# A planner's account of GpSimd and accumulator reads, and the buffers of memory attention, in a two-block transformer kernel

## Chip, cores and metric

The kernel runs on one core of one Trainium2 chip, as one program. The metric is the time of one execution in microseconds of the device, in the median of the runs.

## What is computed

Two transformer blocks, one after the other, in float32, on 256 tokens of width 1024. The first block has two layers, the second has one. Each layer is a mixer and a feed-forward part, each with its RMS norm before it and its residual addition after it.

```python
for layer in range(2):                                   # first block
    u = rms_norm(x, attn_norm_w[layer]) @ w_in[layer]
    o_main = silu(g) * rms_norm(retention(q, k, v))      # layer 0: six heads
    o_main = rms_norm(diff_attention(q, k, v, lam))      # layer 1: q and k normed per 64 columns
    qc = rms_norm(u[..., 3 * MAIN_WIDTH:])               # 4 heads of 64, normed per head
    mk = rms_norm(mem_part_k);  o_mem = softmax(qc @ mk.T / 8) @ mv
    x = x + concat(o_main, o_mem) @ w_out[layer]
    gu = rms_norm(x, ffn_norm_w[layer]) @ w_gate_up[layer]
    x = x + (silu(gu[:FFN]) * gu[FFN:]) @ w_down[layer]
# second block: a state-space mixer and a forgetting attention side by side
# (16 heads each, q and k normed per head), then a gated MLP with a short convolution
```

The memory attention of the two layers of the first block attends from the 256 tokens to 256 memory rows, with four heads.

## The kernel before

**Products.** Every large product is made in three passes of a split: the weights are cast to fp32r (`wh`, on ACT) and the rest is subtracted (`wl`, on VectorE), the activations likewise (`lth`, `ltl`). A unit of weights has 256 rows and 512 columns: one DMA into one of four stage buffers (`st`), one cast, one subtraction. `mm3` issues the three matmuls of one step of 128 rows. Projections accumulate in PSUM banks of the pool `psm` (three of them). All small products, transposes through TensorE and attention use the pool `psa`, which has five banks.

**Stages.** Mixer 0 (retention and memory attention), feed-forward 0, mixer 1 (differential attention and memory attention), feed-forward 1, mixer 2 (state space and forgetting attention), feed-forward 2. In a mixer, the projections of the input run in a fixed order of column chunks (`ORDER0`, `ORDER1`, `ORDER2`), and all the small work of the heads is woven between their matmuls. At the end `w_out` accumulates the output projection over pairs of 128 rows in the order `OUT0`, `OUT1` or `OUT2`, waiting for each pair's heads.

**The planner.** The program is written out by a planner in Python, which decides the order of the instructions before anything runs. `Weave` (line 100 onwards) keeps a modelled clock for each engine; each call to an engine goes through `note` (line 133), which starts the operation at the latest of its engine's clock and its operands' modelled ends and adds `cost` (line 116). Small work is a `Task`, a Python generator. A `yield` hands control back: with nothing, the task may go on at the modelled end of what it has just issued; with a ring and a number, once so many buffers of that ring are free; with tasks, once these are done. `poll` (line 200) runs, after each three matmuls of a projection, all steps whose time has come by the account (100 ns late at the soonest). `join` (line 208) moves TensorE's clock on until the tasks asked for are done. `fill` (line 382) issues weight loads as stage buffers come free, and the casts and subtractions when their operands are there by the account and either the unit is next in turn or ACT's (VectorE's) clock is no more than 100 ns ahead of TensorE's. On the chip each engine takes its instructions in the order in which they were written; semaphores make it wait where an operand is late.

**Rings.** A ring is a set of buffers. A buffer taken with `get(True)` is held until `close`; a free one comes with the modelled end of its last use.

**GpSimd.** Reciprocal roots run on GpSimd, as a tensor_scalar (scale and epsilon) and a tensor_tensor with the power -1/2 (`rsqrt`, line 282, and `stat`, line 479). Tiles with one column (`s1n`) belong to the large norms, with four (`s4r`) to `head_norm` (line 989), with eight (`s8r`) to the memory's keys (`mk`) and queries (`u`), with sixteen (`s16r`) to the heads of differential and forgetting attention (`uq`, `aug`), with two (`s2r`) to the state-space part. In `group_norm64` (line 594) and `head_norm`, a multiplication on VectorE waits for the root, and transposes on TensorE wait for the multiplication.

**ACT's accumulators.** An activation with `accum_out` appears in the profile as two records, the ACTIVATE and an ACTIVATION_READ_ACCUMULATOR. The attentions' exponentials and the squares of the norms have it.

**Memory attention** (`mem_attn`, line 686). After the norm and transposes of the queries, two blocks of 128 tokens run as two tasks, the second started 2.5 us of the account after the first. A block takes two `psa` banks, makes the scores of four heads, takes for each half a buffer of the ring `mpr` (tile `mp`, two buffers in both mixers), writes the exponentials there with their sums, divides, and transposes each half through TensorE into `mpT`, giving back its buffer. When both blocks are done, the product with `mv` follows and its result is split for the output projection.

In the profile all of this has line 89, the helper through which every operation is recorded. The tiles' names tell the operations apart.

Of the kernel before, what the change touches and what calls it, by code (L numbers as in the profile page):

```python
# [10 lines left out]
ALU = mybir.AluOpType  # L11
# [88 lines left out]
class Weave:  # L100
# [15 lines left out]
    def cost(self, key, op, args, kw, aps):  # L116
        n = max(a.size() // a.shape[0] if callable(a.size) else a.size // a.shape[0] for a in aps[:2])
        if key == "T":
            if op == "transpose":
                return 109  # L120
            return n / 2.4 + 3 if args[2].dtype == F32R else max(n / 0.6, 104) + 3
        if key == "V":
            return 65 + 1.05 * n + 60 * any(a.size() == a.shape[0] if callable(a.size) else a.size == a.shape[0] for a in aps[1:])
        if key == "S":
            c = 45 + 0.88 * n + 93 * sum(isinstance(kw.get(k), bass.AP) for k in ("bias", "scale", "accum_out"))
            func = args[2] if op == "activation" else None
            if func in (AF.Exp, AF.Silu) and func != self.table:
                self.table = func
                c += 1280
            return c  # L130
        return 230 + 170 * n if kw.get("op") == ALU.pow else 120 + 2 * n

    def note(self, key, op, args, kw):
        aps = [x for x in list(args) + list(kw.values()) if isinstance(x, bass.AP)]
# [88 lines left out]
def _build(tc, a, out, stop):  # L223
# [13 lines left out]
    def ring(p, n, tag, bufs, dtype=F32):  # L237
        return Ring(W, p, [P] + (list(n) if isinstance(n, (tuple, list)) else [n]), dtype, tag, bufs)
# [103 lines left out]
    def g64(ap):  # L342
        return ap.rearrange("p (g d) -> p g d", d=64)
# [250 lines left out]
    def group_norm64(sq, srcs, dsts, ng):  # L594

        ns = len(srcs)
        ss = small([P, ns, ng], "g")
        for i, s_ in enumerate(srcs):
            yield sq, 1
            q = sq.get(True)  # L600
            S.activation(g64(q[:, : 64 * ng]), s_, AF.Square)
            yield
            V.tensor_reduce(ss[:, i, :], g64(q[:, : 64 * ng]), axis=AX.X, op=ALU.add)
            sq.close(q)
        yield
        r = rsqrt(ss.rearrange("p a b -> p (a b)"), ns * ng, 1.0 / 64)
        yield
        for i in range(ns):
            V.tensor_tensor(dsts[i], srcs[i], bcast(r[:, i * ng : (i + 1) * ng], 64), op=ALU.mult)
        yield  # L610
# [75 lines left out]
    def mem_attn(l, mx, got, kvt, qc, oT, mpr):  # L686

        yield [got]
        qg = [g64(q_) for q_ in qc]
        yield from group_norm64(sqm[0], qg, qg, 4)  # L690
        yield psa, 1
        ps = psa.get(True)
        transposes(ps, [qc[t][:, p * P : (p + 1) * P] for p in range(2) for t in range(2)])
        yield
        qT = mx.tile([P, 2, 256], F32, tag="mqT", name=W.name("mqT"))
        S.activation(qT[:].rearrange("p a b -> p (a b)"), ps[:], AF.Copy, scale=pc(C_MQ + l))
        psa.close(ps)
        yield [kvt]
        v, kT = kvt.val
        sums = small([P, 2, 4], "m")  # L700
        pT = mx.tile([P, 2, 4, 256], F32, tag="mpT", name=W.name("mpT"))

        def block(t):
            yield psa, 2
            sc = [psa.get(True), psa.get(True)]
            for p in range(2):
                for j in range(2):
                    T.matmul(sc[j][:, p * 256 : (p + 1) * 256], qT[64 * j : 64 * j + 64, p, t * P : (t + 1) * P],
                             kT[64 * j : 64 * j + 64, p, :], start=True, stop=True)
            prs = []  # L710
            yield
            for j in range(2):
                mxv = small([P, 2])
                V.tensor_reduce(mxv, sc[j][:].rearrange("p (j m) -> p j m", j=2), axis=AX.X, op=ALU.max)
                V.tensor_scalar(mxv, mxv, -0.125, None, op0=ALU.mult)
                yield mpr, 1
                pr = mpr.get(True)
                for p in range(2):
                    S.activation(pr[:, p * 256 : (p + 1) * 256], sc[j][:, p * 256 : (p + 1) * 256], AF.Exp,
                                 bias=mxv[:, p : p + 1], scale=0.125, accum_out=sums[:, t, 2 * p + j : 2 * p + j + 1])  # L720
                psa.close(sc[j])
                prs.append(pr)
            yield
            rs = small([P, 4])
            V.reciprocal(rs, sums[:, t, :])
            yield
            for j in range(2):
                for p in range(2):
                    cols = slice(p * 256, (p + 1) * 256)
                    S.activation(prs[j][:, cols], prs[j][:, cols], AF.Copy, scale=rs[:, 2 * p + j : 2 * p + j + 1])  # L730
            yield
            for j in range(2):
                yield psa, 1
                tp = psa.get(True)
                transposes(tp, blocks(prs[j]))
                mpr.close(prs[j])
                S.copy(pT[:, j, :, t * P : (t + 1) * P], g128(tp[:]))
                psa.close(tp)
            yield

        b0 = go(block(0))
        yield 2500
        b1 = go(block(1))
        yield [b0, b1]
        yield psa, 1
        ps = psa.get(True)
        for p in range(2):
            for mb in range(2):
                for j in range(2):
                    h = (2 * p + j) * 64  # L750
                    T.matmul(ps[64 * j : 64 * j + 64, p * 256 : (p + 1) * 256], v[mb][:, h : h + 64], pT[:, j, 2 * p + mb, :],
                             start=mb == 0, stop=mb == 1)
        yield
        lt = yield from lt_tiles()
        yield from split(lt[0][:], lt[1][:], ps[:])
        psa.close(ps)
        for t in range(2):
            for p in range(2):
                oT[6 + p, t] = tuple(z[:, (2 * p + t) * P : (2 * p + t + 1) * P] for z in lt)
        yield  # L760
        return [lt]
# [246 lines left out]
    def mixer0(H, nxt, first):  # L1008
        scope = ExitStack()
        mx = scope.enter_context(tc.tile_pool(name="m0", bufs=1))  # L1010
        w = a["w_in"][0]
        u, E, oT = {}, {}, {}
        dtab = mx.tile([P, 6, 384], F32, name="dtab")
        sTr, hsq, onr, mpr = ring(mx, 384, "sT", 3), ring(mx, 512, "hsq", 1), ring(mx, 512, "on", 3), ring(mx, 512, "mp", 2)
        sqm[0] = ring(mx, 256, "sqm", 2)

        def chunk(c, ev, first=None):
# [112 lines left out]
    def mixer1(H, nxt, kv1):  # L1130
        scope = ExitStack()
        mx = scope.enter_context(tc.tile_pool(name="m1", bufs=1))
# [1 line left out]
        oT, u, qkT, E = {}, {}, {}, {}  # L1134
        btab = mx.tile([P, 384], F32, name="btab")
        uqr, sqg, pdr, aTr = ring(mx, 512, "uq", 4), ring(mx, 512, "sqg", 1), ring(mx, 384, "pd", 6), ring(mx, 384, "aT", 5)
        hsq, onr, mpr = ring(mx, 512, "hsq", 1), ring(mx, 512, "on", 2), ring(mx, 512, "mp", 2)
        sqm[0] = ring(mx, 256, "sqm", 1)

        def chunk(c, serial=False):  # L1140
# [748 lines left out]
```

## Time and profile before

| | |
|---|---|
| runs, median (lowest to highest) | 1014.52 us (1013.83 to 1016.05), 3 runs |
| the profiled execution: its own time | 1014.46 us |
| its span, first to last instruction | 1012.5 us |
| TensorE busy | 1002.2 us, 99% |
| VectorE busy | 678.1 us, 67% |
| ACT busy | 622.5 us, 61% |
| GpSimd busy | 69.8 us, 7%, 93 instructions |
| HBM | 191 GB/s over the span |

Busy times are of one profiled execution. A record of a matmul overlaps with the next one's, so the distance of two begins is the time that a matmul takes from TensorE's queue, and not the record's length. Idle time is time in which no record of an engine runs. TensorE is called PE, VectorE DVE and GpSimd POOL in the profile.

### The profile page before, as it was taken

To read this page: it belongs to the slowest core of one execution; us is meant where nothing else is said; L and a number is where in the kernel's file an instruction comes from. 1 tells how busy PE (TensorE), PEld (TensorE's weight loads), DVE (VectorE), ACT (ScalarE), POOL (GpSimd) and SP (SyncE) were. 2 spreads that over 40 slices of the span, in tenths; PEclk is the share of its full clock that TensorE was granted. 3 is DMA by queue.
4 is the path that set the end of the run, shared out by engine and by line. 5 is a ranking of instruction groups with operands and counts; after the bars stand their busy time and mean duration, and the time that the engine had idled before them with its cause. 6 is when DMAs were issued, how large, how long until landed. Compare 5 with 4: busy or idle time off the path is not lost.

```text
span 1012.5 us, 13836 instructions
## 1 busy us (share of the span) xinstructions
PE 1002.2 (99%) x4994; PEld 832.4 (82%) x4994; DVE 678.1 (67%) x1026; ACT 622.5 (61%) x1001; POOL 69.8 (7%) x93
## 2 busy tenths in 40 slices
PE   8999999999999999999999999999999999999998
PEld 6887888888898777788888888888888888888887
DVE  5675666555556877756565477778767667878775
ACT  7558654443455887644445356688778557767853
POOL 1121000000001231100000001100400010000000
PEclk9999999999999999999999999999999999999999
DMA  7763566776564433677677457633632659877743
GB/s 250 261 222 105 183 208 212 252 229 193 179 227 155 146 104 107 208 247 233 203 229 239 137 152 220 215 104 104 210 125 84 208 164 289 262 232 240 247 156 116
DMA packets 121780, 193.79 MB, mean 191 GB/s; under 512 B 8400, under 2 KB 39920, under 8 KB 121584
## 3 DMA queue, kind: packets, MB, share of 16 engines
q1 hardware_dynamic: 121712, 192.92, 59.9%
q8 instruction: 39, 0.64, 0.3%
q14 instruction: 29, 0.24, 0.1%
HBM read 183.43 MB, written 9.45 MB: 191 GB/s over the span
## 4 chain that ended last, share of the span: by engine, by line
PE 91%; ACT 2%; DVE 2%; DMA 2%; POOL 2%; issue 1%; SPq 0%; ACTq 0%; DVEq 0%
PE psm L89 60%; PE psa L89 31%; POOL s8r L89 1%; DMA xt<-x 1%; ACT pd L89 1%; DMA dc<-am 1%; DMA st<-w_gate_up 1%; DVE wl L89 0%; DVE pd L89 0%; DVE s L89 0%; ACT wh L89 0%; POOL s4r L89 0%; POOL s16r L89 0%; SPq L259 0%; ACT qkT L89 0%
## 5 line engine op out<-in xcount | busy, mean ns | idle before, releaser
L89 DVE TENSOR_TENSOR wl<-st,wh 128x1024 fp32r<-128x1024 f32 (+2 forms) x339 | 388.4, 1166 | 195.4 <-ACT wh L89 194.5
L89 ACT CAST wh<-st 128x1024 fp32r<-128x1024 f32 (+2 forms) x339 | 334.5, 1007 | 223.9 <-PE psm L89 84.0
L89 PE MATMUL psm<-wh,lth 128*128 128x512 f32 (+2 forms) x1024 | 395.2, 386 | 1.1 <-ACT lth L89 1.1
L89 PE MATMUL psm<-wl,lth 128*128 128x512 f32 (+2 forms) x1024 | 385.6, 377 | 0.0
L89 PE MATMUL psm<-wh,ltl 128*128 128x512 f32 (+2 forms) x1024 | 381.0, 377 | 0.3 <-DVE ltl L89 0.2
L89 PEld LDWEIGHTS psm<-wh,ltl 128*128 128x128 f32 x1024 | 192.6, 188 | 36.8 <-DVE ltl L89 0.9
L89 PEld LDWEIGHTS psm<-wh,lth 128*128 128x128 f32 x1024 | 192.8, 188 | 35.8 <-issue 2.0
L89 PEld LDWEIGHTS psm<-wl,lth 128*128 128x128 f32 x1024 | 192.9, 188 | 32.6 <-DVE wl L89 0.7
L89 PE MATMUL psa<-wh,lth 128*128 128x512 f32 x328 | 130.7, 398 | 0.0
L89 PE MATMUL psa<-wl,lth 128*128 128x512 f32 x328 | 127.9, 390 | 0.0
L89 PE MATMUL psa<-wh,ltl 128*128 128x512 f32 x328 | 105.1, 390 | 0.0
L89 PEld LDWEIGHTS psa<-wh,ltl 128*128 128x128 f32 x328 | 61.6, 188 | 13.2
L89 PEld LDWEIGHTS psa<-wh,lth 128*128 128x128 f32 x328 | 61.6, 188 | 12.4 <-ACT lth L89 0.3
L89 PEld LDWEIGHTS psa<-wl,lth 128*128 128x128 f32 x328 | 61.7, 188 | 12.0 <-issue 0.2
L89 POOL TENSOR_SCALAR s1n<-s1n 128x1 f32<-128x1 f32 x14 | 5.6, 402 | 461.6 <-ACT sq L89 461.4
L89 DVE SCALAR_TENSOR_TENSOR cc<-na,ccol,cc 128x255 f32<-128x255 f32 (+1 forms) x64 | 27.4, 480 | 7.4 <-ACT cc L89 7.2
L89 ACT ACT_TABLE_LOAD x20 | 25.7, 1283 | 7.8 <-DMA dc<-am 2.8
L89 DVE SCALAR_TENSOR_TENSOR sg<-psm,s1n,sg 128x512 f32<-128x512 f32 (+1 forms) x24 | 16.9, 705 | 19.5 <-PE psm L89 19.3
L89 ACT ACTIVATE uu<-psm,s1n 128x512 f32<-128x512 f32 (+1 forms) x24 | 15.6, 652 | 18.3 <-PE psm L89 18.2
L89 ACT ACTIVATE sg<-psm,s1n 128x512 f32<-128x512 f32 (+1 forms) x24 | 15.7, 653 | 17.9 <-PE psm L89 17.7
L89 ACT ACTIVATE sq<-xt 128x512 f32<-128x512 f32 x24 | 15.2, 634 | 18.2 <-DVE xt L89 17.7
L89 POOL TENSOR_TENSOR s16r<-s16r,mhalf 128x16 f32<-128x16 f32 x7 | 22.2, 3166 | 0.6
(213 smaller groups left out, 829.3 us busy)
## 6 DMA issues: line engine op xcount, KB each, us to landing
st<-w_gate_up SPq DMA_DIRECT2D x80, 512.0 KB, 4.6
st<-w_in SPq DMA_DIRECT2D x67, 512.0 KB, 4.3
st<-w_down SPq DMA_DIRECT2D x66, 512.0 KB, 5.5
st<-w_up SPq DMA_DIRECT2D x40, 512.0 KB, 4.8
st<-w_out SPq DMA_DIRECT2D x32, 512.0 KB, 3.9
scr<-sq SPq DMA_DIRECT2D x64, 128.0 KB, 4.8
fl<-scr SPq DMA_DIRECT2D x16, 512.0 KB, 5.9
st<-w_in SPq DMA_DIRECT2D x30, 256.0 KB, 3.8
```

What stands on the lines that cost most here:

```text
L89: f(*args, **kw)
```

## The change

Three edits. In `cost`, an ACT operation with `accum_out` costs 110 ns more; a GpSimd power goes from 230+170n to 380+175n ns for n columns; any other GpSimd operation goes from 120+2n to 450+15n, but for a memset, which costs 120. In `mem_attn`, a block asks for two buffers of `mpr` before it asks for its two banks, where it asked for one buffer at a time after its scores and the maximum. The ring has three buffers in mixers 0 and 1. The program's instructions stay; the planner writes them in the order of the new account.

```diff
@@ Weave.cost
         if key == "S":
             c = 45 + 0.88 * n + 93 * sum(isinstance(kw.get(k), bass.AP) for k in ("bias", "scale", "accum_out"))
+            c += 110 * ("accum_out" in kw)
             func = args[2] if op == "activation" else None
...
-        return 230 + 170 * n if kw.get("op") == ALU.pow else 120 + 2 * n
+        return 380 + 175 * n if kw.get("op") == ALU.pow else 120 if op == "memset" else 450 + 15 * n
@@ mem_attn
         def block(t):
+            yield mpr, 2
+            prs = [mpr.get(True), mpr.get(True)]
             yield psa, 2
             sc = [psa.get(True), psa.get(True)]
...
-            prs = []
             yield
             for j in range(2):
                 mxv = small([P, 2])
...
-                yield mpr, 1
-                pr = mpr.get(True)
+                pr = prs[j]
...
                 psa.close(sc[j])
-                prs.append(pr)
@@ mixer0
-        ..., mpr = ..., ring(mx, 512, "mp", 2)
+        ..., mpr = ..., ring(mx, 512, "mp", 3)
@@ mixer1
-        hsq, onr, mpr = ring(mx, 512, "hsq", 1), ring(mx, 512, "on", 2), ring(mx, 512, "mp", 2)
+        hsq, onr, mpr = ring(mx, 512, "hsq", 1), ring(mx, 512, "on", 2), ring(mx, 512, "mp", 3)
```

## Rows read from the trace of the kernel before

**Rows 1.** The page's head and its first part: busy time of TensorE, share of the span, instructions.

```profile
span 1012.5 us, 13836 instructions
...
PE 1002.2 (99%) x4994; PEld 832.4 (82%) x4994; DVE 678.1 (67%) x1026; ACT 622.5 (61%) x1001; POOL 69.8 (7%) x93
```

**Rows 2.** Busy time by stage: mixer 0 with the start-up, feed-forward 0, mixer 1, mixer 2. After the stretch and its length in us: busy us (and instructions) of PE, PEld, DVE, ACT and POOL, the granted clock, DMA share, GB/s.

```profile
0.00:131.50 131.50, 127.77 (x640) 103.03 (x641) 83.88 (x126) 90.27 (x162) 19.64 (x34) 1.00 0.60 199
131.50:308.40 176.90, 176.90 (x833) 148.27 (x832) 100.55 (x105) 80.90 (x96) 0.99 (x3) 1.00 0.69 219
308.40:420.40 112.00, 109.55 (x581) 86.55 (x580) 85.61 (x156) 85.53 (x186) 24.05 (x24) 1.00 0.44 137
...
597.40:826.90 229.50, 229.17 (x1254) 194.12 (x1253) 170.16 (x335) 166.13 (x300) 23.53 (x30) 1.00 0.50 155
```

**Rows 3.** The chain of work that ended last, at the head of feed-forward 0: start us, us, what, number of matmuls.

```profile
131.55 42.18 PE psm L89 x186
```

**Rows 4.** The waits of TensorE: what waited for whom, us in total, times, longest us. The rows of the start-up are left out.

```profile
PE psa L89 <- DVE u L89: 1.0, 1, 1.0
PE psa L89 <- DVE xt L89: 0.9, 1, 0.9
...
PE psa L89 <- DVE mk L89: 0.4, 1, 0.4
PE psa L89 <- DVE pd L89: 0.3, 1, 0.3
PE psa L89 <- DVE on L89: 0.2, 1, 0.2
```

**Rows 5.** The instructions on the tiles `s4r` and `s16r`: count, duration in ns as minimum/median/maximum, first and last start.

```profile
L89 POOL TENSOR_SCALAR s4r<-s4h x6: 193/200/1102, 43.5 to 400.1; 128x4 f32<-128x4 f32 x6
...
L89 POOL TENSOR_SCALAR s16r<-s16g x7: 205/211/2241, 328.8 to 725.1; 128x16 f32<-128x16 f32 x7
L89 POOL TENSOR_TENSOR s16r<-s16r,mhalf x7: 2899/2911/3861, 329.1 to 727.5; 128x16 f32<-128x16 f32 x7
```

**Rows 6.** Instructions in order of time, mixer 0, around the norm of the memory's keys: start us, us, engine, operation, tiles, number, idle time before and who ended it.

```profile
66.45 2.35 DVE L89 TENSOR_TENSOR wl<-st,wh 128x1024 fp32r<-128x1024 f32 x2
66.63 1.11 POOL L89 TENSOR_SCALAR s8r<-s8g 128x8 f32<-128x8 f32 x1 [5.92 <-DVE s8g L89]
...
70.00 0.39 PE L89 MATMUL psm<-wh,ltl 128*128 128x512 f32 x1
...
70.81 0.95 PE L89 MATMUL psa<-pcol,mk 128*128 128x128 f32 x4 [0.42 <-DVE mk L89]
```

**Rows 7.** The same, mixer 1, around the norm of the memory attention's queries.

```profile
358.52 2.35 DVE L89 TENSOR_TENSOR wl<-st,wh 128x1024 fp32r<-128x1024 f32 x2
...
358.69 2.24 POOL L89 TENSOR_SCALAR s8r<-s8g 128x8 f32<-128x8 f32 x1 [15.34 <-DVE s8g L89]
...
361.90 0.39 PE L89 MATMUL psm<-wh,ltl 128*128 128x512 f32 x1
...
363.26 0.85 PE L89 MATMUL psa<-pcol,u 128*128 128x128 f32 x4 [0.97 <-DVE u L89]
```

**Rows 8.** TensorE in order of time, mixer 0: the scores of the two blocks of memory attention (`kT,mqT`) and the first transposes of each (`pcol,mp`).

```profile
86.25 1.14 PE L89 MATMUL psa<-kT,mqT 64*128 64x256 f32 x8
...
88.21 1.13 PE L89 MATMUL psa<-kT,mqT 64*128 64x256 f32 x8
...
94.19 0.60 PE L89 MATMUL psa<-pcol,mp 128*128 128x128 f32 x4
...
101.75 0.60 PE L89 MATMUL psa<-pcol,mp 128*128 128x128 f32 x4
```

**Rows 9.** ACT in order of time, mixer 1: two exponentials of the memory attention and the accumulator read between them.

```profile
370.76 0.48 ACT L89 ACTIVATE mp<-psa,s 128x256 f32<-128x256 f32 x1
371.12 0.22 ACT L89 ACTIVATION_READ_ACCUMULATOR mp<-psa,s 128x1 f32 x1
371.22 0.49 ACT L89 ACTIVATE mp<-psa,s 128x256 f32<-128x256 f32 x1
```

**Rows 10.** The groups of instructions: ACT's table loads, number, busy us and mean ns, idle time before them and what ended most of it.

```profile
L89 ACT ACT_TABLE_LOAD x20 | 25.7, 1283 | 7.8 <-DMA dc<-am 2.8 <-PE psm L89 2.8 <-DVE s L89 1.2
```

**Rows 11.** TensorE in order of time, mixer 1: scores and transposes of the memory attention's blocks, and the two transposes of one chunk of queries and keys (`pcol,uq`).

```profile
367.14 1.14 PE L89 MATMUL psa<-kT,mqT 64*128 64x256 f32 x8
...
370.44 1.13 PE L89 MATMUL psa<-kT,mqT 64*128 64x256 f32 x8
...
373.03 0.60 PE L89 MATMUL psa<-pcol,mp 128*128 128x128 f32 x4
...
374.17 0.60 PE L89 MATMUL psa<-pcol,uq 128*128 128x128 f32 x4
...
377.30 0.60 PE L89 MATMUL psa<-pcol,uq 128*128 128x128 f32 x4
...
382.92 0.60 PE L89 MATMUL psa<-pcol,mp 128*128 128x128 f32 x4
```

**Rows 12.** ACT and VectorE in order of time at the end of mixer 1, before the residual addition (`xt`) for which TensorE waits.

```profile
409.73 1.05 ACT L89 CAST wh<-st 128x1024 fp32r<-128x1024 f32 x1 [1.58 <-DMA st<-w_gate_up]
410.82 1.23 DVE L89 TENSOR_TENSOR wl<-st,wh 128x1024 fp32r<-128x1024 f32 x1 [1.41 <-ACT wh L89]
411.96 1.28 DVE L89 TENSOR_TENSOR xt<-psm,xt 128x512 f32<-128x512 f32 x2
```

More of the change, by code (lines that the diff above doesn't have):

```diff
@@ L1013, in mixer0 @@
         dtab = mx.tile([P, 6, 384], F32, name="dtab")
-        sTr, hsq, onr, mpr = ring(mx, 384, "sT", 3), ring(mx, 512, "hsq", 1), ring(mx, 512, "on", 3), ring(mx, 512, "mp", 2)
+        sTr, hsq, onr, mpr = ring(mx, 384, "sT", 3), ring(mx, 512, "hsq", 1), ring(mx, 512, "on", 3), ring(mx, 512, "mp", 3)
         sqm[0] = ring(mx, 256, "sqm", 2)
```

## Prediction

> **What bounds the kernel now.** I read the busy shares and the slices first, then the stages, then the waits of TensorE, and last the places of those waits in order of time. TensorE is busy 1002.2 of 1012.5 us, at a granted clock of 1.00 of full speed (the upper level, 2.4 GHz) in every stage [rows 1, 2]. In the first feed-forward stretch it is busy for the whole 176.9 us, and there 186 matmuls of 512 columns take 42.18 us, 0.227 us each, end to start [rows 2, 3]. So nothing off TensorE costs time there. The three mixers are where other engines can be late: TensorE idles 3.7 us in mixer 0 (its share of the start-up among it), 2.45 us in mixer 1 and 0.33 us in mixer 2 [rows 2]. The waits have names: `u` 1.0, `xt` 0.9, `mk` 0.4, `pd` 0.3 and `on` 0.2 us [rows 4]. Together that is 2.8 us of idle time. This is the ceiling of any new order of the same instructions, but for what a late operand stretches in the matmuls after it.
>
> The change gives no engine less work. It alters the planner's account, and so the order in which the same instructions stand in each queue. A step is placed when its input is ready by the account; TensorE's queue is in order, so a transpose that is placed too early stops everything behind it.
>
> **GpSimd's account.** Each reciprocal root is a tensor_scalar and a power. For n columns the pair went in as (120+2n)+(230+170n) ns and now goes in as (450+15n)+(380+175n): 1.04 to 1.59 us for n=4, 1.73 to 2.35 for n=8, 3.10 to 3.87 for n=16, so 0.55, 0.62 and 0.77 us more. The rows say something less simple than "longer". The tensor_scalar's median is 0.20 us at n=4 and 0.21 at n=16, and its maxima are 1.10 and 2.24; the power takes 2.91 at n=16, and at most 3.86 [rows 5]. Undisturbed, n=16 is 0.21+2.91 = 3.12 us, the old account to 0.02 and 0.75 below the new one. The long ones are those of rows 6 and 7: the tensor_scalar of 66.63 ends with the first of two `wl` subtractions that VectorE began at 66.45, the one of 358.69 lasts 2.24 us, just until the pair of `wl` begun at 358.52 (2.35 us) is over [rows 6, 7].
>
> The Trainium skill (SBUF — State Buffer, "Who interferes with whom") has it that a VectorE instruction with two SBUF inputs contends with a GpSimd instruction that reads SBUF, and that whichever comes first blocks the other for its whole length; this trace agrees, with the 2.24 us above. That rule speaks against the change, for by it no constant is right: the pair is short or long by what VectorE does beside it. By it alone the result would be that of rival (b), 1014.4 us; by the rows and the longer account it is the sum's 1012.8.
>
> What the longer account moves: after a root the multiplication on VectorE and the transposes on TensorE come later. TensorE looks for ready steps after every three matmuls, 0.68 us [rows 3], so 0.62 us more is one place, as a rule. For `mk`: the transposes stood due 0.23 us after the matmul of 70.00 and began at 70.81, 0.58 us late; the four took 0.95 where four undisturbed ones take 0.60 [rows 6, 8]: 0.93 us in all. One place later leaves 0.25, a gain of 0.68. For `u`: due at 362.13, begun at 363.26, and 0.85 instead of 0.60: 1.38 us [rows 7]. One place later leaves 0.70, a gain of 0.68; two places, a gain of 1.38. For `on` (n=4, 0.55 us more) the 0.2 us goes, with some stretch 0.3. Bounds of this edit: a gain of 2.6 us if all three vanish, nothing if the new places meet new blocked roots. I take 0.68+0.68+0.3 = 1.66 us. The later steps behind them are covered by projections, whose matmuls are ready to fill; where that cover is gone, at the end of a mixer, a place costs its 0.68 us.
>
> **The accumulator reads.** The account of an ACT operation with accum_out grows by 110 ns. In mixer 1 one Exp of 256 columns begins at 370.76 and the next at 371.22, 0.46 us apart; the read of the first ends at 371.34, 0.58 us after its begin [rows 9]. The old account is 45+225+186 = 456 ns, the pitch; the new one is 566 ns, the completion. So those who wait for a sum or a row of probabilities are now placed about right, and ACT's queue is booked 0.10 us too long for each. Bounds: a gain of 0.3 (the `pd` wait), a loss by casts of weights that are placed later, the third rival. I take nothing: ACT has cover, 85.5 us busy of 112 in mixer 1 [rows 2], and a shift of 0.1 us is below a place. The order of Exp and Silu may also change the number of table loads, now 20 of 1.28 us [rows 10], on ACT alone; nothing, under the same cover. Memsets go from 136 to 120 ns: nothing.
>
> **Three buffers, ahead of the banks.** Today the second block of the memory attention takes two of the five `psa` banks at 88.21 and 370.44, and then has no `mp` buffer until the first block's transposes (94.19, 373.03) [rows 8, 11]. Its own transposes come at 101.75 and 382.92. The new block asks for two buffers first; of three, one is left, so it begins when the first block gives back one, at about 94.5 and 373.3, and holds no bank before. The banks are free for some 6 and 3 us more. In mixer 1 the second `uq` transpose, at 377.30, 3.1 us after the first at 374.17 [rows 11], asks for a bank in that time; if it comes earlier, the last pair of heads does too. The second block becomes later: the first took 7.9 us from scores to transposes (86.25 to 94.19) [rows 8], so from 94.5 the second has its own at about 102.4, 0.7 us after today's; in mixer 1 (first block 367.14 to 373.03, 5.9 us) at about 379.2, 3.7 us before [rows 11]. What waits is a step of the planner, not an instruction, so nothing queues behind it on an engine, and the steps that move issue no DMA; SP's queue changes only by the place of the weight loads, which follow the free stage buffers. Bounds: the 1.2 us of `xt` and `pd` as a gain, and 0.7+0.62 us as a loss if mixer 0's output projection has no filler. I take zero: no wait of TensorE stands for `mp` or its result [rows 4].
>
> **The sum.** Profiled execution: 1014.46 us for a span of 1012.5, so 2.0 lie around it; the median of the runs is 1014.52, the same. 1014.46 − 1.66 = 1012.8 us, 0.16% less. Something like 0.2%, 2.0 us, is the least that a measurement of this kernel can tell from no change; so the likeliest result is a small gain at its edge.
>
> **The rivals.** (a) *Whole gain.* The account makes the steps fit and the freed banks bring the tail of mixer 1 forward: `u` 1.38, `mk` 0.93, `on` 0.3, and the idle time of `xt` and `pd`, 0.9+0.3: 3.8 us, 1010.7. For it: the waits are all in the stretches that move. Against it: `xt` waits for an addition that stands behind a weight subtraction on VectorE, behind a cast, behind a load [rows 12], and the change touches none of these. (b) *The account says nothing of the chip.* Blocked roots depend on which `wl` runs beside them; a new order meets others, and the gain is given back: 1014.4. For it: rows 6 and 7 and the medians of rows 5. Against it: even a wrong constant places the two worst steps later. (c) *Slower: weights come late.* ACT is booked 0.1 us too long for each accumulator and casts are placed only when ACT is free by the account (or the unit is next in turn); then `wl`, and behind it the VectorE queue, is late at the ends of the mixers, as `xt` is now. Its price is one cast and one subtraction, 1.05+1.23 us at most [rows 12], about half of it in sight of TensorE (`xt` now: 0.9 idle): 1.2 us in each of three mixers, 3.6 less the 1.66: 1016.4. It decides when ACT's account runs more than one cast ahead of TensorE's at a mixer's end, where no projection is left as cover. (d) *The order is the same.* Impossible in full, since the second block must move, but if the places don't change where TensorE waits: 1014.5, counted with (b).
>
> **How the numbers follow.** The forecast's case has 0.42, with a spread of 1.4 us either way, because one place more or less at two sites is that much; a bit over a third of it, 0.16, lies beyond 2.0 us of gain. Rival (a) has 0.20, (b) and (d) together 0.22, (c) 0.16, nearly all of it above +0.2%. Faster by over 0.2%: 0.16+0.20+0.02 = 0.38. Slower: 0.14 from (c), 0.01 from (b): 0.15. Within: 0.47. The range reaches from (a) and 0.4 below to just short of (c): 1010.3 to 1016.0.
>
> **What would show it.** Right: the wait for `u` falls below 0.7 us and that for `mk` to about 0.2; the multiplications after the roots wait less for GpSimd; the second block's scores follow the first block's transposes; the feed-forward stretches last as long as before. Rival (a) shows as no wait of TensorE over 0.3 us between 60 us and the end of mixer 1; (b) as roots blocked by other `wl` and new waits for `aug`, `uq` or `on`; (c) as ACT's casts ended by other work than DMA and longer waits for `wl` or `xt` at the ends of the mixers. A shift of more than 5 us either way would refute the ceiling, and with it the whole argument.

## The result and the profile after

The changed kernel took 1025.15 us in the median of 4 runs (1023.99 to 1026.10), the kernel before 1015.09 in 4 runs beside them: a ratio of 1.010, with an interval of 1.008 to 1.012. The forecast was 1012.8, its range ended at 1016.0. The profiled execution spans 1023.0 us, 10.5 more than in [rows 1]. The page's head and the head of its first part, after:

```profile
span 1023.0 us, 13843 instructions
...
PE 1006.0 (98%) x4994; PEld 835.1 (82%) x4994; DVE 677.6 (66%) x1026; ACT 624.9 (61%) x1003; POOL 68.5 (7%) x93
```

TensorE has the same 4994 matmuls and is busy 3.8 us longer; the other 6.7 us are new idle time. By stage, after, with the columns of [rows 2] (mixer 0 with the start-up, feed-forward 0, mixer 1, mixer 2, feed-forward 2):

```profile
0.00:139.39 139.39, 131.82 (x640) 105.56 (x641) 83.63 (x126) 92.13 (x164) 20.00 (x34) 0.98 0.57 188
139.39:316.20 176.81, 176.81 (x833) 148.20 (x832) 100.58 (x105) 80.95 (x96) 0.94 (x3) 1.00 0.68 219
316.20:429.60 113.40, 109.16 (x577) 86.19 (x576) 84.75 (x156) 84.82 (x185) 23.31 (x23) 1.00 0.43 133
...
607.00:837.00 230.00, 229.88 (x1262) 195.54 (x1261) 171.72 (x337) 166.46 (x301) 23.19 (x31) 1.00 0.51 156
837.00:1023.00 186.00, 180.90 (x852) 150.71 (x850) 137.05 (x198) 118.56 (x163) 0.00 (x0) 1.00 0.68 218
```

The rows of after for mixer 2 and feed-forward 2 are cut at 837.00, 1.7 us behind the stage's end at 835.27, while that of before is cut 0.3 us behind it; so mixer 2 looks too long in them and feed-forward 2 too short. Between one marker in both kernels (the first matmul of a stage's own products) the stages changed by +7.84 (mixer 0), +0.02, +1.94 (mixer 1), −0.02, −1.13 (mixer 2) and +1.88 us (feed-forward 2), 10.53 together. Mixer 0 is three quarters of the loss: by its rows, 3.84 us more idle time (7.57 against 3.73), and 4.05 us more busy time for the same 640 matmuls. The largest waits of TensorE after, with the columns of [rows 4]:

```profile
PE psa L89 <- DVE ltl L89: 4.0, 1, 4.0
PE psa L89 <- DVE on L89: 1.7, 1, 1.7
...
PE psa L89 <- ACT lth L89: 1.3, 1, 1.3
PE psa L89 <- ACT u L89: 1.3, 2, 0.8
```

The waits for `u` and `xt` of VectorE are gone, the one for `mk` too. The 4.0 us are in mixer 0, the 1.7 for `on` in mixer 1, the 1.3 for `lth` in feed-forward 2. The wait for a `u` of ACT is new, in two pieces at 392.33 and 393.49 in mixer 1.

**Mixer 0, the start of the chain.** The roots of the queries and what follows, after, in order of time (columns as in [rows 6]):

```profile
79.55 0.21 POOL L89 TENSOR_SCALAR s8r<-s8g 128x8 f32<-128x8 f32 x1 [9.49 <-DVE s8g L89]
79.84 1.64 POOL L89 TENSOR_TENSOR s8r<-s8r,mhalf 128x8 f32<-128x8 f32 x1
...
82.01 1.22 DVE L89 TENSOR_TENSOR wl<-st,wh 128x1024 fp32r<-128x1024 f32 x1 [0.64 <-ACT wh L89]
83.15 0.75 DVE L89 TENSOR_TENSOR u<-u,s8r 128x256 f32<-128x256 f32 x2
83.64 1.05 ACT L89 CAST wh<-st 128x1024 fp32r<-128x1024 f32 x1 [1.67 <-PE psm L89]
85.46 0.48 ACT L89 ACTIVATE mk<-psm,s1n 128x256 f32<-128x256 f32 x1 [0.77 <-PE psm L89]
...
86.19 0.69 ACT L89 ACTIVATE mqT<-psa,pcol 128x512 f32<-128x512 f32 x1
```

The pair of roots takes 1.93 us, to 81.48; the new account says 2.35, so the multiplication stands behind one more subtraction (`wl`) and begins 1.67 us after the root. The same three steps before:

```profile
80.74 1.64 POOL L89 TENSOR_TENSOR s8r<-s8r,mhalf 128x8 f32<-128x8 f32 x1
...
82.41 0.76 DVE L89 TENSOR_TENSOR u<-u,s8r 128x256 f32<-128x256 f32 x2
...
84.30 0.69 ACT L89 ACTIVATE mqT<-psa,pcol 128x512 f32<-128x512 f32 x1 [1.43 <-PE psa L89]
```

There it began 0.03 us after the root's end (82.38), and the copy `mqT` 1.92 us after; now the copy is 4.71 us after, behind a cast and two evacuations (of `mk` and `mv`) that were placed ahead of it. Measured from the first projection, the scores come 2.1 us later.

**Mixer 0, the two blocks.** TensorE after, as in [rows 8], and one row of before that answers to the last:

```profile
88.07 1.13 PE L89 MATMUL psa<-kT,mqT 64*128 64x256 f32 x8
...
97.35 0.60 PE L89 MATMUL psa<-pcol,mp 128*128 128x128 f32 x4
...
98.58 1.14 PE L89 MATMUL psa<-kT,mqT 64*128 64x256 f32 x8
...
108.64 0.84 PE L89 MATMUL psa<-pcol,mp 128*128 128x128 f32 x4 [0.61 <-ACT mp L89]
113.45 1.09 PE L89 MATMUL psa<-pcol,mp 128*128 128x128 f32 x4 [3.98 <-DVE ltl L89]
114.47 4.42 PE L89 MATMUL psa<-mpT,mv 128*64 128x256 f32 x16
```

```profile
106.71 1.95 PE L89 MATMUL psa<-mpT,mv 128*64 128x256 f32 x16
```

Before, the scores were 1.96 us apart; now 10.51, and the product with `mv` begins 7.8 us later. From there to feed-forward 0 it is 24.6 us before and 24.7 after. What ACT does between the blocks, after:

```profile
98.59 1.28 ACT L89 ACT_TABLE_LOAD   x1
99.89 0.69 ACT L89 ACTIVATE u<-psm,s1n 128x512 f32<-128x512 f32 x1
...
101.07 1.28 ACT L89 ACT_TABLE_LOAD   x1
102.36 0.47 ACT L89 ACTIVATE mp<-psa,s 128x256 f32<-128x256 f32 x1
...
104.31 1.28 ACT L89 ACT_TABLE_LOAD   x1
...
106.20 1.98 ACT L89 CAST wh<-st 128x1024 fp32r<-128x1024 f32 x2
108.08 1.71 ACT L89 ACTIVATE mp<-mp,s 128x256 f32<-128x256 f32 x4
109.69 1.98 ACT L89 CAST wh<-st 128x1024 fp32r<-128x1024 f32 x2
111.57 1.55 ACT L89 ACTIVATE lth<-psa,pcol 128x256 fp32r<-128x256 f32 x4
```

The gate's Silu (`u`) falls between the exponentials of the two blocks, so the table is changed to Silu, back to Exp and to Silu again: 22 loads in the program instead of 20 [rows 10]. Behind them stand casts, the scaling, casts, and then the split of the last heads, whose `ltl` gives back the bank for which the last transposes wait 3.98 us. The queue of TensorE is in order, so nothing else goes on. The last 38 us of mixer 0, after and then before:

```profile
101.00:139.15 38.15, 32.89 (x155) 25.56 (x153) 21.01 (x31) 24.89 (x46) 1.87 (x4) 0.91 0.37 115
```

```profile
93.00:131.31 38.31, 38.31 (x199) 30.98 (x198) 24.02 (x36) 28.81 (x54) 3.71 (x6) 1.00 0.41 129
```

199 matmuls ran in that time before and 155 now: the products that used to cover the memory attention had been used up ahead of it. The first products of the output projection stood behind the product with `mv` before (from 109.00); now they stand ahead of it (from 104.27). That is how a mixer gets longer with the same instructions.

**Mixer 1 and feed-forward 2.** In mixer 1 the last pair of heads is late (its second pair of `uq` transposes at 386.48, 1.3 us later by the stage's own time [rows 11]), and TensorE waits for it near the end. The waits of TensorE in this stage add up to 4.2 us, against 2.3 before, which is nearly all of the +1.94. The longest:

```profile
415.38 0.66 PE L89 MATMUL psa<-pcol,on 128*128 128x128 f32 x4 [1.67 <-DVE on L89]
```

In feed-forward 2 the casts `lth` of the convolution's result stand behind three weight casts and two evacuations, and TensorE waits 1.28 us (ACT and one row of TensorE, after):

```profile
873.02 3.08 ACT L89 CAST wh<-st 128x1024 fp32r<-128x1024 f32 x3
...
877.76 0.69 ACT L89 ACTIVATE uu<-psm,s1n 128x512 f32<-128x512 f32 x1 [0.67 <-PE psm L89]
878.35 1.13 ACT L89 CAST lth<-cc 128x512 fp32r<-128x512 f32 x2
...
879.01 0.50 PE L89 MATMUL psa<-wh,lth 128*128 128x512 f32 x1 [1.28 <-ACT lth L89]
```

### The profile page after: what moved, and what is told of

It is laid out like the page before. It is cut to its first block, busy times and chain, and to the rows that moved or that the text cites. A ratio compares the mean times of both kernels' runs of the same rounds, so it can differ in the third digit from the quotient of the medians.

```text
span 1023.0 us, 13843 instructions
## 1 busy us (share of the span) xinstructions
PE 1006.0 (98%) x4994; PEld 835.1 (82%) x4994; DVE 677.6 (66%) x1026; ACT 624.9 (61%) x1003; POOL 68.5 (7%) x93
## 4 chain that ended last, share of the span: by engine, by line
PE 95%; ACT 2%; DVE 1%; DMA 1%; issue 0%; SPq 0%; POOL 0%; ACTq 0%
PE psm L89 64%; PE psa L89 31%; DMA xt<-x 1%; ACT mp L89 0%; ACT wh L89 0%; ACT L89 0%; ACT pd L89 0%; ACT lth L89 0%; SPq L260 0%; ACT mpT L89 0%; POOL s4r L89 0%; DVE ltl L89 0%; ACT u L89 0%; DVE pd L89 0%; DVE wl L89 0%
## 5 line engine op out<-in xcount | busy, mean ns | idle before, releaser
L89 ACT ACT_TABLE_LOAD x22 | 28.2, 1283 | 6.5 <-PE psm L89 2.8
```

The lines of the kernel that those rows point to most:

```text
L89: f(*args, **kw)
```

## The experiments

The theory was that the new account and order delay the memory attention of mixer 0, which had next to no slack, and that the mixer's end follows it. The rivals were that one edit alone costs all of it, that the two table loads do, or the order of the output projection, or TensorE's clock. The table gives all runs. "Mixer 0" is counted from its first long run of projections, so that differences of the start-up stay out; the stage columns are changes in us against the profile of before (119.5, 111.8, 230.2 and 185.9).

| kernel | median us | ratio (95%) | mixer 0 | mixer 1 | mixer 2 | ff 2 |
|---|---|---|---|---|---|---|
| the change | 1025.15 | 1.010 (1.008 to 1.012) | +8.2 | +1.9 | −1.1 | +1.9 |
| e1_gpsimd | 1030.22 | 1.0153 (1.0138 to 1.0168) | +8.2 | +7.4 | −1.0 | 0.0 |
| e3_order3 | 1029.42 | 1.0141 (1.0124 to 1.0158) | +1.8 | +11.2 | +0.8 | +0.2 |
| e12_acc_ring3 | 1024.92 | 1.0107 (1.0092 to 1.0122) | +6.6 | +2.8 | −1.1 | +2.3 |
| e13_after_four | 1028.07 | 1.0130 (1.0115 to 1.0145) | +1.4 | +12.2 | −1.2 | +1.7 |
| f1_gps_mix2 | 1013.54 | 0.9991 (0.9982 to 1.0000) | +0.1 | +0.2 | −1.0 | +0.4 |
| f2_after_notable | 1021.73 | 1.0069 (1.0055 to 1.0082) | +4.6 | +2.0 | −1.2 | +1.4 |
| f3_gps_only8 | 1023.02 | 1.0082 (1.0068 to 1.0096) | +8.0 | +0.1 | +0.8 | +0.1 |
| f4_after_out0 | 1023.82 | 1.0094 (1.0080 to 1.0107) | +7.4 | +2.0 | −1.2 | +1.5 |
| f5_after_silu_late | 1022.31 | 1.0076 (1.0059 to 1.0093) | +5.7 | +2.9 | −1.1 | +1.9 |
| g1_both_mix2 | 1014.80 | 1.0004 (0.9995 to 1.0013) | +0.2 | −0.2 | −1.2 | +2.3 |
| g2_after_warm | 1023.81 | 1.0092 (1.0077 to 1.0107) | +7.0 | +2.0 | −1.2 | +1.8 |
| g3_after_not8 | 1031.86 | 1.0171 (1.0156 to 1.0186) | +6.1 | +10.8 | −1.1 | +1.4 |
| h1_after_kvlast | 1022.78 | 1.0080 (1.0065 to 1.0095) | +4.6 | +3.0 | −1.1 | +1.4 |
| h2_before_kvlast | 1015.59 | 1.0012 (1.0002 to 1.0022) | +1.4 | −0.1 | −0.5 | +1.0 |

**Each part alone.** e1_gpsimd is the kernel before with GpSimd's account; e3_order3 is it with the buffers ahead of the banks and three of them; e12_acc_ring3 is the changed kernel with the old order of requests; e13_after_four is it with four buffers, and smaller rings `sT` and `sqm` in mixer 0.

```diff
# e1_gpsimd (on the kernel before)
-        return 230 + 170 * n if kw.get("op") == ALU.pow else 120 + 2 * n
+        return 380 + 175 * n if kw.get("op") == ALU.pow else 120 if op == "memset" else 450 + 15 * n
# e3_order3 (on the kernel before): the edits in mem_attn and the two rings, old accounts
# e12_acc_ring3 (on the changed kernel)
-            yield mpr, 2
-            prs = [mpr.get(True), mpr.get(True)]
...
-                pr = prs[j]
+                yield mpr, 1
+                pr = mpr.get(True)
# e13_after_four (on the changed kernel), mixer 0
-ring(mx, 384, "sT", 3), ..., ring(mx, 512, "mp", 3); sqm[0] = ring(mx, 256, "sqm", 2)
+ring(mx, 384, "sT", 2), ..., ring(mx, 512, "mp", 4); sqm[0] = ring(mx, 256, "sqm", 1)
```

> The kernel before with GpSimd's new account alone. Theory A (the buffers ahead of the banks make the second block of memory attention late, and mixer 0's output projection waits for it): no late second block here, 1012 to 1015 us, the stage up to feed-forward 0 about 131.5 us as before, TensorE's waits for u and mk shorter. Rival B (the longer accounts push memory attention late, the buffers do little): most of the loss is here already, 1019 us or more, mixer 0 at 136 us or more.

> The kernel before with the memory attention's edit alone: three buffers, two of them asked for ahead of the banks, old accounts. Theory A: the second block's scores follow the first block's transposes, mixer 0 ends 5 to 8 us later than before, 1019 to 1023 us in all. Rival B: 1013 to 1016 us, mixer 0 within 1 us of before.

> Both accounts as in the changed kernel and three buffers, but a block asks for its buffers one at a time after its banks, as before. Theory A: the two blocks overlap again, mixer 0 within 1.5 us of the kernel before, 1012 to 1017 us in all. Rival B: mixer 0 stays 5 us or more late, 1020 to 1025 us.

> The changed kernel with four buffers instead of three, so that both blocks get two at once; to make room in mixer 0, its rings of retention scores and of squares for the small norms have one buffer less. Theory A: the second block's scores come about 2.5 us after the first's again, the gap of TensorE of some 7 us in mixer 0 is gone, 1013 to 1019 us. Rival B: as the changed kernel, 1023 to 1026 us.

GpSimd's account alone and the buffers alone each cost more than all three edits together; the accumulators' account alone was not run from the start. GpSimd's account alone gives mixer 0 its whole +8.2, although the scores of its two blocks are 1.95 us apart, as before; the buffers alone give +1.8 there and +11.2 in mixer 1; with the old order of requests mixer 0 is still +6.6. So the parts don't add up, and no one edit is the cause.

e13_after_four came out as its first theory said in mixer 0 (+1.4) and as neither said in mixer 1 (+12.2). Its mixer 0 is the telling one: the scores begin 2.9 us late, counted from the first projection, later than in the changed kernel, but the exponentials and the scaling of both blocks are over at 102.07, ahead of the load for the gate's Silu (102.09), and the product with `mv` is 2.8 us late instead of 8.1. So a late start need not cost the 8 us. Over these runs the mixer follows that product: it begins 8.1 us late in the changed kernel (mixer 0 +8.2), 8.2 in e1_gpsimd (+8.2), 7.0 in e12_acc_ring3 (+6.6) and 2.1 in e3_order3 (+1.8).

Mixer 1's large losses are of the kind of mixer 0's. TensorE at the end of mixer 1 in e3_order3:

```profile
410.15 1.49 PE L89 MATMUL psa<-pcol,pd 128*128 128x128 f32 x6 [1.73 <-DVE pd L89]
...
411.96 2.93 PE L89 MATMUL psa<-u,aT 128*128 128x128 f32 x12 [0.31 <-ACT aT L89]
...
418.39 0.89 PE L89 MATMUL psa<-pcol,on 128*128 128x128 f32 x4 [3.51 <-DVE on L89]
```

The last pair of heads runs with nothing beside it and TensorE waits for its steps. The granted clock is at half, 1.2 GHz, for 3.4 us from 411.85, and the 12 products in that time take 2.93 us, where the last 12 take 1.50 in the kernel before (at 397.12).

**Which roots, and where.** f3_gps_only8 gives the kernel before the new account for the roots of eight columns alone; f1_gps_mix2 gives it the whole GpSimd account, but from mixer 2 on; g1_both_mix2 adds the accumulators' account there; g3_after_not8 is the changed kernel with the old account for eight columns.

```diff
# f3_gps_only8 (on the kernel before)
+        if n == 8:
+            return 380 + 175 * n if kw.get("op") == ALU.pow else 120 if op == "memset" else 450 + 15 * n
# f1_gps_mix2 (on the kernel before); W.late is set ahead of mixer 2
+        if self.late:
+            return 380 + 175 * n if kw.get("op") == ALU.pow else 120 if op == "memset" else 450 + 15 * n
# g1_both_mix2: f1_gps_mix2 and
+            c += 110 * (self.late and "accum_out" in kw)
# g3_after_not8 (on the changed kernel)
+        if n == 8 and op != "memset":
+            return 230 + 170 * n if kw.get("op") == ALU.pow else 120 + 2 * n
```

> The kernel before, with GpSimd's new account for tiles of eight columns alone (the norms of memory attention's keys and queries). Theory A (mixer 0's loss comes from the memory attention's norm being placed later): mixer 0, from the first long run of projection matmuls to the feed-forward, 5 to 9 us over before, as with the whole GpSimd account. Rival B (the loss needs the other roots too): under 2 us over before.

> The kernel before, with GpSimd's new account from mixer 2 on alone; the order up to there is that of before. Theory A (a longer account pays where nothing at a stage's end hangs on the steps it moves): mixers 0 and 1 as before, mixer 2 about 1.1 us shorter, 1013 to 1014 us. Rival B (the account is worth nothing anywhere, mixer 2's gain in the other runs came with the different entry into it): 1014.5 us, mixer 2 within 0.3 us of before.

> The kernel before, with both new accounts (GpSimd's operations and ACT's accumulator reads) from mixer 2 on alone; the memory attention as before. Theory A (the accumulator reads' account makes feed-forward 2 longer): feed-forward 2 about 1.5 to 2 us over before, mixer 2 about 1.1 us under it, 1014 to 1016 us. Rival B (feed-forward 2's loss comes from the state that the earlier stages leave): within 0.5 us of before there, 1013 to 1014 us.

> The changed kernel with GpSimd's old account for tiles of eight columns (the norms of memory attention), all else as changed. Theory A (that account alone pushes the second block behind the gate's Silu): mixer 0 within 3 us of before, three table loads there instead of five, 1017 to 1020 us. Rival B (the buffers asked for ahead of the banks, or the accumulators, are enough to push it): mixer 0 6 us or more over before, 1023 us or more.

0.62 us more for each of four pairs of roots, of which mixer 0 has three, make mixer 0 8.0 us longer (the only other edit is 16 ns less for memsets of eight columns): the account of the roots of eight columns is enough. It is not necessary: g3_after_not8 without it still loses 6.1 us there, and 10.8 in mixer 1, so the theory that this account is the cause fell as far as that. In its mixer 0 the scores start as before and no table load is added, but the second block's transposes come 4.1 us later. The new order of requests alone does not do that, as they are 0.6 us later in e3_order3, which has it too. The difference is in ACT's order: in g3_after_not8 the load for the Silu, a `u` and `kT` stand between the second block's exponentials and its scaling (101.31 to 103.75), in e3_order3 the load and the `u` come behind the scaling (104.45).

From mixer 2 on GpSimd's account does what it was forecast to do at the start: −1.0 us in mixer 2, and a median 0.09% below that of before, with no change just inside the interval. Little of the gain is a wait of TensorE that ended: its idle time in mixer 2 fell from 0.33 to 0.12 us, and the same 1230 matmuls were busy 223.55 us instead of 224.37. It is not the table loads either, of which f1_gps_mix2 has four fewer than before, since g1_both_mix2 has as many as before and gains the same. What makes the matmuls closer there was not tried. With the accumulators' account, mixer 2 is the same, and feed-forward 2 has the 1.28 us wait for `lth` of the changed kernel. In f1_gps_mix2 ACT's order there is another:

```profile
865.17 1.06 ACT L89 CAST wh<-st 128x1024 fp32r<-128x1024 f32 x1 [0.97 <-PE psm L89]
866.53 0.69 ACT L89 ACTIVATE uu<-psm,s1n 128x512 f32<-128x512 f32 x1 [0.30 <-PE psm L89]
867.12 1.13 ACT L89 CAST lth<-cc 128x512 fp32r<-128x512 f32 x2
868.15 0.69 ACT L89 ACTIVATE uu<-psm,s1n 128x512 f32<-128x512 f32 x1
```

The casts `lth` come between the two `uu` there, and behind both with the accumulators' account. That edit costs 1.9 us (+2.3 against +0.4), at a place where I had looked for nothing.

**The table loads and the gate.** f2_after_notable copies the gate instead of taking its Silu, in an unchanged order (the Silu is left out); f5_after_silu_late takes the Silu in place when both blocks are done; h1_after_kvlast projects the gate ahead of the second memory chunk; h2_before_kvlast makes that exchange in the kernel before.

```diff
# f2_after_notable; the planner still counts a Silu
-        chunk(3, lambda t, ps, r: S.activation(u[3, t][:], ps[:], AF.Silu, scale=r))
+            nc.scalar.activation(u[3, t][:], ps[:], AF.Copy, scale=r)
# f5_after_silu_late
+        chunk(3, copy_ev(3))
...
+            while len(blks) < 2 or not all(b.done for b in blks):
+                yield 500
+            for t in range(2):
+                S.activation(u[3, t][:], u[3, t][:], AF.Silu)
# h1_after_kvlast, h2_before_kvlast; join(kv1) moves to the mixer's end
-    ORDER0, OUT0 = (0, 1, 2, "kv0", 4, "kv1", 3), (4, 6, 0, 2)
+    ORDER0, OUT0 = (0, 1, 2, "kv0", 4, 3, "kv1"), (4, 6, 0, 2)
```

> The changed kernel with the gate of chunk 3 in mixer 0 evacuated by a copy instead of Silu, the account and so the order unchanged: no Silu stands between the second block's exponentials, so two of ACT's table loads (1.28 us each) go and nothing else moves. The gate's Silu is left out of the result. Theory A (the pair of loads in the chain of memory attention is a good part of mixer 0's loss): mixer 0 is 2.5 to 5 us shorter than in the changed kernel, 1020 to 1022.5 us. Rival B (the chain is late by the order of casts and by GpSimd's account, the loads are covered): less than 1 us, 1024 to 1025 us.

> The changed kernel with chunk 3 of mixer 0 evacuated by a copy and its Silu made in place when both blocks of the memory attention are done: two operations of ACT more, no table load between the exponentials. Theory A (Silu between the blocks is what lengthens the chain): mixer 0 3 to 6 us shorter than in the changed kernel, 1019 to 1022 us. Rival B (the gate is late then, and the heads of retention wait in its place): no shorter, 1024 us or more.

> The changed kernel with the last chunk of mixer 0 (the gate) projected ahead of the second memory chunk, whose keys and values are waited for at the mixer's end. Nothing is left out. Theory A (the memory attention of the changed order meets the gate's Silu on ACT, with two more table loads, and the retention heads that wait for it): the gate is done before the exponentials, two table loads fewer, and mixer 0 is at least 4 us shorter than in the changed kernel's 127.7 us. Theory B (the memory attention is the last chain of the mixer in any order): its keys and values now come later still by the length of a chunk's product, some 14 us, less what lies between; mixer 0 is as long as in the changed kernel or longer. Mixers 1 and 2 as in the changed kernel.

> The kernel before with the same exchange of the two last chunks of mixer 0, and nothing of the change. Theory A: no gain of note, since in the kernel before the exponentials and the Silu do not cross; mixer 0 within 2 us of its 119.5 us. Theory B: mixer 0 longer by more than 4 us, because its last chain starts later.

With the same order and two table loads fewer, mixer 0 is 3.6 us shorter than in the changed kernel: that is the price of the crossing in this order, the wait for `ltl` included, which falls from 3.98 to 2.04 us. h1_after_kvlast gives back the same 3.6 us in another way, its Silu being done before the exponentials. It stops at +4.6, a little short of what its first theory asked for. Its second theory had a wrong premise: the second memory chunk holds the keys and values of mixer 1, so the attention here does not wait for them. But the moved chunk brings a wait of its own (TensorE, h1_after_kvlast):

```profile
110.14 2.69 PE L89 MATMUL psa<-mpT,mv 128*64 128x256 f32 x16
...
115.79 0.80 PE L89 MATMUL psa<-pcol,mk 128*128 128x128 f32 x4 [2.96 <-DVE mk L89]
```

f5_after_silu_late starts the product with `mv` 2.8 us after the time of before, yet loses 5.7: there the retention heads, which need the gate, are last, and TensorE waits 3.26 us for `on`. h2_before_kvlast shows that the exchange itself costs little, +1.4 in mixer 0. Its premise, that exponentials and Silu do not cross there, was wrong: one `u` stands between the first block's exponentials (91.88), with two loads more than before, 22 in all. So a crossing has no fixed price: there the whole exchange, crossing included, costs 1.4 us.

**The order of the output and the clock.** f4_after_out0 takes the memory attention's pair last in the output projection; g2_after_warm gives TensorE 20 matmuls of ones ahead of the last transposes, into a bank that nobody reads.

```diff
# f4_after_out0
-    ... (4, 6, 0, 2)
+    ... (4, 0, 2, 6)
# g2_after_warm, in the second block of mixer 0
+                    for _ in range(20):
+                        nc.tensor.matmul(wb[:], onesr[:], rep(onesr[:], 4), start=True, stop=True)
```

> The changed kernel with mixer 0's output projection in the order 4, 0, 2, 6, so that the memory attention's rows come last instead of second. Theory A (the output projection stands still for the memory attention alone): at least half of mixer 0's loss is covered by the work of pairs 0 and 1, mixer 0 3 to 7 us shorter, 1018 to 1022 us. Rival B (the heads of retention are as late as the memory attention): the gap stays, 1024 us or more.

> The changed kernel with twenty matmuls of ones into a free bank of psm, placed in TensorE's queue ahead of the last transposes of mixer 0's memory attention, where it waits some 4 us. They feed nothing. Theory A (after the wait TensorE runs at half its clock, and that lengthens the products behind it): the granted clock stays at full, the sixteen products with mv take about 2 us instead of 5, mixer 0 2 to 3 us shorter, 1021.5 to 1023.5 us. Rival B (those products wait for ACT's copies whatever the clock): the clock stays at full and mixer 0 loses less than 1 us, 1024 to 1026 us.

With the memory attention's pair last, 0.8 us come back of 8.2: the transposes and the product with `mv` stand in TensorE's queue ahead of what could fill. Keeping the clock up gives back 1.2 us, short of the 2 to 3 of the first theory; the 20 matmuls themselves make the last transposes 0.45 us later. TensorE in g2_after_warm:

```profile
109.50 4.83 PE L738 MATMUL psm<-ones 128*128 128x512 f32 x20
...
114.70 2.69 PE L89 MATMUL psa<-mpT,mv 128*64 128x256 f32 x16
```

In the changed kernel the granted clock is at half, 1.2 GHz, from 112.0 us for 6.8 us; it falls within the wait, which began at 109.5 and ended at 113.45. Here it stays at 2.4 GHz, and the 16 products take 2.69 us instead of 4.42.

## Why the prediction was wrong

**The step that failed.** It is the sentence that later steps "are covered by projections", and that at a mixer's end, where the cover is gone, "a place costs its 0.68 us". The cover is a fixed stock of matmuls; the planner hands them out in order, and when a step is late it uses them earlier, until the last 38 us of mixer 0 hold 155 instead of 199. And a place is not 0.68 us. One place of the account for eight columns (f3_gps_only8) became one more subtraction ahead of the multiplication, a cast and two evacuations ahead of `mqT`, 2.8 us at the scores (2.1 in the changed kernel), and then the Silu between the exponentials. The loss is 8.0 us, twelve places. How much of it is the Silu was not tried in that kernel; in the changed one it is 3.6 us, and in e13_after_four, where the scores are as late and no Silu comes between, the whole loss is 1.4.

**GpSimd's account: the gains came and were outweighed.** The waits for `u` and `mk` are gone, which the prediction priced at 2.31 us with what they stretch, and of which it took 1.36. The wait for `on`, from which it took the other 0.3, grew from 0.2 to 1.7 us. The operations that read a root of eight columns wait less. Who waited for `s8r`, before and then after (us, times):

```profile
  DVE mk L89: 2.8, 2
  DVE u L89: 1.4, 1
```

```profile
  DVE mk L89: 0.4, 1
```

Over the roots of four and sixteen columns, too, VectorE's waits fall, from 7.7 to 2.3 us. In mixer 2 the gain of 1.0 to 1.2 us appears in every kernel with this account and in none without it. The forecast put the gains into mixers 0 and 1, where the same account cost more. Rival (b) is not borne out: the readers of roots wait less in the new order, and do not only meet other subtractions. That this is what makes mixer 2 shorter is not shown, as no wait of TensorE for a root shows there. In mixer 0 itself, though, the root ran undisturbed in 1.93 us, between the old account (1.73) and the new (2.35): too long an account is not a safe side.

**The accumulator reads: nothing taken, 1.9 us lost.** The step looked at mixers and bounded the loss by casts at their ends. The loss is in feed-forward 2, by the casts `lth`, which moved from behind one evacuation to behind two. "The feed-forward stretches last as long as before" held for two of three.

**The table loads: "nothing, under the same cover".** They cost, with the Silu's place, 3.6 us in mixer 0 (f2_after_notable), since ACT had become the engine on which the end of the mixer hung. The page "ScalarE: Activation LUTs" of the Trainium skill (What ACT_TABLE_LOAD costs) gives a switch as about 1283 ns for the load and 1380 more for a drain. The trace agrees on the load, 1.28 us; the second half does not show, as the load begins at 98.59, 0.01 us after the copy before it ends, and the Silu at 99.89, 0.02 us after the load is over.

**Three buffers ahead: right in kind, wrong in size.** The second block's scores do follow the first block's transposes, by 1.2 us. The forecast had its transposes at 102.4; they came at 108.64 and 113.45. Of the first 6.2 us, 1.8 are the later start of the first block, 1.3 its length (9.28 us instead of 7.94), 0.9 the longer way from its transposes to the second block's scores, and 2.2 the length of the second (10.06 instead of 7.9), with two table loads inside it. Done one after the other, the blocks add up what they had shared. That no wait of TensorE stood for `mp` before was no proof of slack; it showed that the planner had placed the steps late enough.

**The ceiling.** Idle time of TensorE (2.8 us) was taken as the ceiling of any change, with 5 us as what would refute it. The shift was 10.1 us. Idle time can bound gains at most, and not even those strictly: mixer 2 had 0.33 us of it and became 1.0 us shorter in f1_gps_mix2. Losses it doesn't bound: I costed rival (c) at 1.2 us for a mixer. Its sign came true; its mechanism did not, as the wait for `xt` at the mixers' ends vanished.

**What stays open.** Why mixer 1 loses 1.9 us with all edits and 7 to 12 with some of them is not settled beyond the place: in all of these the last pair of heads is late and TensorE waits for it (3.5 us for `on` in four of them). Which placement decides it was not tried. Both ways of removing the crossing from the changed order, f2_after_notable and h1_after_kvlast, leave 4.6 us in mixer 0. The later start of the scores is not all of that: e13_after_four has it, with the blocks overlapping again and no Silu between, and loses 1.4. Blocks one after the other with a start as before lose 1.8 (e3_order3). No run changes one of the two alone in the changed order, and e13_after_four has smaller rings besides. The best version found is f1_gps_mix2, if its 0.09% is real.

## What to carry to other kernels

In a kernel whose order is written by a planner, the slack of the last chain of each stage is to be looked up before the account is changed: here the memory attention's product with `mv` stood 24.6 us ahead of the next stage, and each us later was about a us of time. Work that covers is a stock: count the matmuls left in the last stretch of a stage, before and after, to see whether a late step can still be hidden. An account closer to the mean of the measured durations can still make a worse order: for a power of sixteen columns the new one says 3.18 us and the old one 2.95, and the mean before was 3.17. So put it in stage by stage, as f1_gps_mix2 did, and near a stage's end keep activations of different tables from crossing.

## What was not expected of the hardware

Within a wait of 3.98 us the granted clock of TensorE fell to half for 6.8 us, and 16 small products took 4.42 us, where they took 1.95 before and 2.69 with the clock kept up. 20 matmuls of no use in the wait kept it at 2.4 GHz and gave back 1.2 us of the 8.2. At the end of mixer 1 in e13_after_four the half clock lasted 13.7 us, with the waits for `pd` (3.9 us) and `on` (3.5 us) around it: a late chain of small steps pays for its waits a second time.
